# Down projections of two groups per feed-forward block: two of four pairs by seven products, added from PSUM to the residual; constants loaded per mixer

## The chip, the cores and the metric

The kernel runs on one core of one Trainium2 chip. The metric is device time in microseconds (us). Before the change it is 2205.03 us, the median of three runs between 2204.33 and 2206.0 us.

## The reference

Input is x, 512 tokens of 1024 channels, before which 16 learned meta tokens stand (528 tokens in all). Two layers (DEPTH = 2) each apply a feed-forward block, a mixer and a second feed-forward block:

```python
for l in range(DEPTH):
    h = h + 0.5 * swiglu(rmsnorm(h, norm_gains[l, 0]), ffn_w_gate[l, 0], ffn_w_up[l, 0], ffn_w_down[l, 0])
    h = h + mixer(rmsnorm(h, norm_gains[l, 1]), w_in[l], ...)
    h = h + 0.5 * swiglu(rmsnorm(h, norm_gains[l, 2]), ffn_w_gate[l, 1], ffn_w_up[l, 1], ffn_w_down[l, 1])
return rmsnorm(h, final_norm)[:, N_META:]

def swiglu(x, w_gate, w_up, w_down):
    return (jax.nn.silu(x @ w_gate) * (x @ w_up)) @ w_down
```

The inner width of a feed-forward block is 2816. The mixer joins a gated linear attention and a softmax attention. All of it is float32.

## The kernel before, in words

**Layout.** Channels lie on the 128 partitions, tokens on the free axis; the residual h stays on the chip as eight chunks of 128 channels by 528 tokens (`hall`). After the mixer of the last layer only the 512 real tokens are kept, so in the last feed-forward block a half of the tokens has 256 columns instead of 264. A float32 matmul is made of three: every operand is split into a high part (`hi`, rounded to the format `fp32r`) and a low part (`lo`, the remainder), and high x high, high x low and low x high are added in PSUM.

**Weights.** They come from DRAM in slabs of 128 x 1024 floats (512 KB). `Weights.fetch` loads up to six slabs ahead on SP's queue into three `raw` buffers; `Weights.make` converts up to four ahead: ScalarE casts to `whi` (L283), VectorE forms the remainder `wlo` (L284); there are four buffers of each. `fetch` and `make` set the order of the program; a scheduler then orders each engine's queue by that order and by its estimate of when operands and buffers are ready.

**Gate and up.** The 22 hidden chunks of a block are worked on as 11 pairs, in groups of 4, 4 and 3 (`GROUPS`). For a pair, the gate and up projections are done by a seven-product scheme in place of eight block products: rows of the input (even and odd chunks) and halves of the tokens are the two-by-two blocks of the one operand, the pair's two hidden chunks and the rows those of the weights. The products are named "1", "2", "5", "6", "7", "4", "3"; each has its own slab and takes 24 matmuls (L671). "1", "2" and "4" use slabs as they are; the others use sums of slabs that `Weights.sums` makes: a negated copy on ScalarE (L231) and transfers on POOL's queue that add what they carry to their target (L236). Buffers for that are three long ones (`wsa`) and three short ones (`wsb`). The seven sums of the input (`Norm.pair`) lie in `xc`.

**PSUM.** All eight banks are two pools of two tiles of two banks, `ss` and `s2`; pairs take turns between them. A product's result that is both used and added to further is copied from PSUM by ScalarE (`snapshot`, L683, three buffers `snap`), and VectorE adds a second accumulator to it (L692, L697, L701) in a buffer `c` (two of them, one per pair, taken at product "2").

**Hidden rows.** `hidden` scales the gate half by the norm's factor rs (L712), applies SiLU (L438) and multiplies it with the up half (L721); the up half is scaled by rs in the last group only (L719). Then the row is split into high and low (L443, L444), in 16 buffers `g`. A row m = 1 follows product "4", a row m = 0 product "3".

**Down.** After a group, `down` computes for each of the 8 output chunks the sum over the group's hidden chunks (L455 by `product`): 384 matmuls of half of the tokens for a group of four pairs, or 192 of all 512 tokens in the last block. In the first two groups `add_to_h` scales the result by rs into a buffer (L591) and adds that to h (L600); in the last group it adds from PSUM (L596). The first chunks begin before the last pair's hidden rows are ready, and take these last.

**The first block** differs at its start: pairs 0 and 1 use plain block products (`first_pair`, L625), while the sums of the input are still being made, and their four hidden rows follow together once rs is known.

**Constants.** Rotary tables, an identity and small matrices (721 KB, `ct`) and a mask are loaded once, on ScalarE's queue, during pair 5 of the first block (L388). The mixer begins with `decay_weights` (L1147 to L1151), which loads a 256 KB weight and splits it by a column of the constants; four gate rows with SiLU, the low-rank product (L1163) and two pairs of heads follow. Its first reader of the decay weights is the matmul in L813, which feeds the scan in L823.

Of the kernel before, what the change touches and what calls it, by code (L numbers as in the profile page):

```python
# [17 lines left out]
P = 128  # L18
# [24 lines left out]
GROUPS = (4, 4, 3)  # L43
HELD = 4
# [20 lines left out]
CONSTANTS_AT = 5  # L65
# [3 lines left out]
DIRECT = {"1": "11", "2": "12", "4": "22", **{b: b for b in BLOCKS}}  # L69


def ffn_steps(begin):
# [4 lines left out]
    for g, n in enumerate(GROUPS):  # L77
# [6 lines left out]
        for i in range(n):  # L84
            p, more = pair + i, i + 1 < n
            early = [[("P", p + 1, "1")], [("P", p + 1, "2")]] if more else \
                [[("D", g, 0, 0, 2 * n - 2)], [("D", g, 1, 0, 2 * n - 2)]]
            if begin and p < 2:
                continue
            if g == 0 and i == 0:  # L90
                early = [[], []]
            steps += early[0] + [("P", p, "7")] + early[1] + [("P", p, "4"), ("P", p, "3")]
            if more:
                steps += [("P", p + 1, "6"), ("P", p + 1, "5")]
# [7 lines left out]
def weight_plan():  # L102
# [8 lines left out]
    def ffn(l, f):  # L111
        for step in ffn_steps((l, f) == (0, 0)):
# [4 lines left out]
            elif step[0] == "F":  # L117
                plan.extend(("op", (l, f), step[1], step[2] + c) for c in "12")
            else:
# [41 lines left out]
NPAIR = FF // P // 2  # L161
# [39 lines left out]
class Weights:  # L201
# [3 lines left out]
    def __init__(self, nc, after, raw, hi, lo, wts, win):  # L205
        self.nc, self.raw, self.hi_pool, self.lo_pool, self.wts, self.win = nc, raw, hi, lo, wts, win
# [8 lines left out]
        self.made, self.fetched, self.got, self.summed, self.raws = 0, 0, {}, {}, {}  # L215
        self.pos, self.behind, self.after = 0, None, after

    def dram(self, f, i, name):
        return self.win[((f[0] * 2 + f[1]) * NPAIR + i) * 4 + BLOCKS.index(name)]

# [17 lines left out]
    def sums(self, f, i, product, w):  # L238
# [3 lines left out]
        if product == "1":  # L242
# [4 lines left out]
            got[f, i, "7"], got[f, i, "6"] = s3, s2  # L247
        else:
            s1 = self.block(f, i, "21", self.short, "wsb")
            self.add(s1, self.dram(f, i, "22"))  # L250
            s4 = self.negative(f, i, "s4", w)
            self.add(s4, got[f, i, "6"])
            got[f, i, "5"], got[f, i, "3"] = s1, s4
# [37 lines left out]
    def use(self, j):  # L291
# [3 lines left out]
        self.make(upto)  # L295
# [18 lines left out]
    def op(self, *load):  # L314

        assert PLAN[self.pos][1:] == load, (PLAN[self.pos], load)
        self.pos += 1
        return [t.rearrange("p (w k m) -> p w k m", w=2, k=KC // 2) for t in self.use(self.at[load])]


def build(tc, ctx, xt, wts, win, par, w2, const, umask, out):
# [16 lines left out]
    W = Weights(nc, after, pool("wraw", 3), pool("whi", 4), pool("wlo", 4), wts, win)  # L338
# [45 lines left out]
    ct = one.tile([P, NCONST], F32, name="const")  # L384
    mask = one.tile([P, P], U32, name="mask")
    nc.sync.dma_start(front[:, : KC + T], xt[:, : KC + T])
    def load_constants():
        S.dma_start(ct, const)  # L388
        S.dma_start(mask, umask)

# [3 lines left out]
    cos, sin = ct[:, C_COS : C_COS + T], ct[:, C_SIN : C_SIN + T]  # L394
    ident = ct[:, C_ID : C_ID + P]
# [6 lines left out]
    b64, diag2 = ct[:, C_B64 : C_B64 + P], ct[:, C_DIAG : C_DIAG + P]  # L402
# [190 lines left out]
    def add_to_h(m, acc, rs, f):  # L593
        if rs is None:
            for pv, cut in acc.parts:
                V.tensor_tensor(cut(h(m)), cut(h(m)), pv, ALU.add)  # L596
        else:
            t = slot("t")
            scaled(t, acc, rs, f)
            V.tensor_tensor(h(m), h(m), t, ALU.add)  # L600

    pending, kept = [load_constants], []

    def ffn(l, f, norm, done, following):
# [3 lines left out]
        pools = kept.pop() if kept else open_pools("left", psum=("s2",), c=2, snap=3, s2=2)  # L608
        made, hid, sums = {}, {}, {}

        def second(p):
            return (p + f) % 2 == 0

        factor = []

        def first_pair(p, m):
# [14 lines left out]
            if "c" not in st:  # L631
                st["c"] = slots["c"].tile([P, 4 * T], F32, tag="c", name=nm("c"))[:, : 4 * n] \
# [760 lines left out]
```

## Time and profile before

| | |
|---|---|
| runs | 2204.33, 2205.03, 2206.0 us |
| profiled execution, first to last instruction | 2203.2 us |
| matmuls | 16572 |
| slab casts by ScalarE (`whi`) | 219 + 190 + 84, about 1.05 us each |
| slab remainders by VectorE (`wlo`) | 219 + 190 + 84, about 1.22 us each |
| additive transfers on POOL's queue | 4 x 42, 512 KB each |

PE is TensorE's matmuls, PEld its weight loads, DVE VectorE, ACT ScalarE, POOL GpSimd, SP SyncE. A row of the chain in order of time gives start, duration and a run of like instructions. A row of the timeline gives start, duration, engine, line and operation, tiles written and read, sizes, count, and in brackets the idle time before it with what ended it. A row of groups gives the count, the busy time and mean ns of one, then the idle time just before. Feed-forward blocks lie at 0 to 372, 768 to 1122, 1122 to 1484 and 1849 to 2203 us; the mixers between.

### The profile page before, as it was taken

To read this page: it belongs to the slowest core of one execution; us is meant where nothing else is said; L and a number is where in the kernel's file an instruction comes from. 1 tells how busy PE (TensorE), PEld (TensorE's weight loads), DVE (VectorE), ACT (ScalarE), POOL (GpSimd) and SP (SyncE) were. 2 spreads that over 40 slices of the span, in tenths; PEclk is the share of its full clock that TensorE was granted. 3 is DMA by queue.
4 is the path that set the end of the run, shared out by engine and by line. 5 is a ranking of instruction groups with operands and counts; after the bars stand their busy time and mean duration, and the time that the engine had idled before them with its cause. 6 is when DMAs were issued, how large, how long until landed. Compare 5 with 4: busy or idle time off the path is not lost.

```text
span 2203.2 us, 39894 instructions
## 1 busy us (share of the span) xinstructions
PE 2184.4 (99%) x16572; PEld 2091.6 (95%) x16572; DVE 1510.3 (69%) x2401; ACT 1214.3 (55%) x1820; POOL 147.3 (7%) x172
## 2 busy tenths in 40 slices
PE   9999999999999999999999999999999999999998
PEld 9999999999999999999999999999888888989897
DVE  7656567577876686565786575675879867656565
ACT  8535355355784574453585363554557847536354
POOL 0011000000000010101010110000000001101010
PEclk9999999999999999999999999999999999999999
DMA  8578553211113585866677685632211146868562
GB/s 251 156 177 228 145 143 111 80 60 65 39 39 125 133 224 151 197 168 174 174 186 194 172 211 147 160 110 78 68 66 60 40 134 165 237 158 225 148 168 67
DMA packets 87286, 310.22 MB, mean 141 GB/s; under 512 B 9665, under 2 KB 11841, under 8 KB 87105
## 3 DMA queue, kind: packets, MB, share of 16 engines
q1 hardware_dynamic: 61120, 217.15, 28.8%
q0 software_dynamic: 24192, 88.09, 23.0%
q8 instruction: 130, 2.13, 0.4%
q10 hardware_dynamic: 1792, 2.43, 0.4%
q14 instruction: 52, 0.42, 0.1%
HBM read 261.50 MB, written 2.10 MB: 120 GB/s over the span
## 4 chain that ended last, share of the span: by engine, by line
PE 91%; DVE 6%; ACT 2%; issue 1%; DMA 0%; DVEq 0%; SPq 0%; ACTq 0%
PE ss L671 38%; PE ss L455 28%; PE mm L455 13%; PE sm L455 3%; PE ss L625 2%; PE sm L1083 1%; PE ss L653 1%; PE ss L1057 1%; DVE wlo L284 1%; ACT t L438 1%; PE sm L1101 1%; PE sm L1102 1%; PE ss L1058 1%; DVE t L823 1%; PE sm L899 0%
## 5 line engine op out<-in xcount | busy, mean ns | idle before, releaser
L671 PE MATMUL ss<-xc,whi 128*128 128x264 f32 (+1 forms) x4608 | 837.3, 284 | 0.0
L671 PEld LDWEIGHTS ss<-xc,whi 128*128 128x128 f32 x4608 | 711.9, 188 | 1.3 <-ACT snap L683 0.5
L671 PE MATMUL ss<-xc,wlo 128*128 128x264 f32 (+1 forms) x2304 | 651.8, 283 | 0.0
L455 PE MATMUL ss<-g,whi 128*128 128x264 f32 (+1 forms) x2620 | 482.5, 300 | 0.0
L671 PEld LDWEIGHTS ss<-xc,wlo 128*128 128x128 f32 x2304 | 433.7, 188 | 0.0
L455 PEld LDWEIGHTS ss<-g,whi 128*128 128x128 f32 x2620 | 380.7, 188 | 15.6
L455 PE MATMUL mm<-x,whi 128*128 128x264 f32 (+1 forms) x1712 | 384.1, 314 | 0.0
L283 ACT CAST whi<-w 128x1024 fp32r<-128x1024 f32 (+1 forms) x219 | 228.8, 1046 | 240.6 <-PE ss L455 116.3
L283 ACT CAST whi<-raw 128x1024 fp32r<-128x1024 f32 x190 | 199.1, 1048 | 263.1 <-PE ss L671 89.7
L284 DVE TENSOR_TENSOR wlo<-w,whi 128x1024 fp32r<-128x1024 f32 (+1 forms) x219 | 265.6, 1217 | 105.0 <-ACT whi L283 102.0
L455 PE MATMUL ss<-g,wlo 128*128 128x264 f32 (+1 forms) x1310 | 301.9, 300 | 0.0
L284 DVE TENSOR_TENSOR wlo<-raw,whi 128x1024 fp32r<-128x1024 f32 x190 | 232.0, 1221 | 90.8 <-ACT whi L283 89.0
L455 PEld LDWEIGHTS mm<-x,whi 128*128 128x128 f32 x1712 | 279.0, 189 | 15.5 <-DVE x L444 0.2
L455 PE MATMUL mm<-x,wlo 128*128 128x264 f32 (+1 forms) x856 | 264.4, 313 | 0.0
L455 PEld LDWEIGHTS ss<-g,wlo 128*128 128x128 f32 x1310 | 209.1, 188 | 8.3
L283 ACT CAST whi<-s 128x1024 fp32r<-128x1024 f32 x84 | 88.2, 1050 | 145.1 <-PE ss L671 126.7
L455 PEld LDWEIGHTS mm<-x,wlo 128*128 128x128 f32 x856 | 160.1, 189 | 7.1
L284 DVE TENSOR_TENSOR wlo<-s,whi 128x1024 fp32r<-128x1024 f32 x84 | 102.7, 1223 | 91.7 <-ACT whi L283 91.7
L231 ACT ACTIVATE s<-w 128x1024 f32<-128x1024 f32 x84 | 89.1, 1061 | 78.8 <-DMA w<-win 49.0
L591 DVE SCALAR_TENSOR_TENSOR t<-ss,rs 128x528 f32<-128x528 f32 (+1 forms) x64 | 44.3, 700 | 126.9 <-PE ss L455 126.8
L236 POOL DMA_DIRECT2D w<-win x42 | 37.0, 882 | 963.4 <-DVE g L1214 739.8
L683 ACT COPY snap<-ss 128x528 f32<-128x528 f32 (+1 forms) x126 | 73.8, 586 | 1.6 <-PE ss L671 1.6
(287 smaller groups left out, 2883.3 us busy)
## 6 DMA issues: line engine op xcount, KB each, us to landing
w<-win SPq DMA_DIRECT2D x217, 512.0 KB, 4.9
raw<-wts SPq DMA_DIRECT2D x190, 512.0 KB, 3.4
w<-win POOLq DMA_DIRECT2D x42, 512.0 KB, 7.6
s<-win POOLq DMA_DIRECT2D x42, 512.0 KB, 6.8
w<-s POOLq DMA_DIRECT2D x42, 512.0 KB, 5.5
s<-w POOLq DMA_DIRECT2D x42, 512.0 KB, 6.6
h<-xt SPq DMA_DIRECT2D x7, 264.0 KB, 5.7
const<-const ACTq DMA_DIRECT2D x1, 721.0 KB, 9.3
```

Of the source, the lines that this page charges most:

```text
L231: self.nc.scalar.activation(t, w, AF.Copy, scale=-1.0)
L236: self.nc.gpsimd.dma_start(t, src, accum_op=ALU.add)
L283: nc.scalar.copy(hi[:, cs], w[:, cs])
L284: nc.vector.tensor_tensor(lo[:, cs], w[:, cs], hi[:, cs].bitcast(F32), ALU.subtract)
L438: prev_act[0] = S.activation(*args, **kw).ins
L455: TE.matmul(acc.half[i][:width], lhs, rhs[:, acc.spans[i]], start=first, stop=last)
L591: V.scalar_tensor_tensor(cut(dst[rows]), pv[rows], -0.5 * f, cut(rs[rows]), ALU.mult, ALU.mult)
L625: last = TE.matmul(acc[:, t, :w], a[:, j, k], v[b][:, r], start=k == 0 and r == 0 and i == 0, stop=k == len(x) - 1 and r == 1 and i == 2)
L653: TE.matmul(acc[:, j], a[:, j, k], b[:, at], start=k == 0 and i == 0, stop=k == last and i == 2)
L671: TE.matmul(acc[:, j], a[:, j, k], b[:, at], start=bool(begin and k == 0 and i == 0), stop=k == len(x) - 1 and i == 2, skip_group_check=no ...
L683: snap = S.copy(st[name], acc).ins
L823: V.tensor_tensor_scan(c[:, bs], ones.broadcast_to([P, n]), g[:, bs], 0.0, ALU.mult, ALU.add)
```

## The change

In the first two groups of every feed-forward block, the first two pairs' share of the down projection is done by seven products too, with the same forms: output rows (even and odd chunks) and halves of the tokens are the blocks. Their hidden rows are not split as they are, but as the seven forms (`forms`), in `g` and a new pool `gx` of six buffers in place of the three `snap`. The other two pairs' share is done by plain products over four slabs per group (`oa`, `ob`, `ea`, `eb`). One group's down stage has eleven steps in the order `SEVEN`, from eleven slabs instead of eight, of which four are sums made as for the gate and up products, with four more additive transfers. Step "1" stands before the last pair's products "4" and "3". Every accumulator is added from PSUM to two chunks of h at a time (`add`, 16 per group), so the hidden rows of all pairs are now scaled by rs in the up half. Copies from PSUM go straight into `c`, which is taken at product "1". The order of the third pair's product "3" and the fourth's "6" is exchanged. The third group and the closing part stay, but for the buffers of the squares. Constants and mask are loaded at the start of each mixer into its own pools, and `decay_weights` moves behind the gate rows and the table load.

```diff
 GROUPS = (4, 4, 3)
+SEVENS = 2
+SEVEN = ("1", "6", "5", "7", "o22", "4", "o21", "ea", "2", "eb", "3")
-CONSTANTS_AT = 5
+SUMMED = [sum(GROUPS[:g]) + i for g in range(SEVENS) for i in range(2)]
...
+            if g < SEVENS and not more:
+                steps += [("P", p, "7"), ("S", g, "1"), ("P", p, "4"), ("P", p, "3")]
+                steps += [("S", g, what) for what in SEVEN[1:]]
+                continue
...
+            if g < SEVENS and i == n - 2:
+                steps += [("P", p, "4"), ("P", p + 1, "6"), ("P", p, "3"), ("P", p + 1, "5")]
...
-        self.make(upto)
+        self.last = j
+        self.make(upto - self.hold)
...
-        pools = kept.pop() if kept else open_pools("left", psum=("s2",), c=2, snap=3, s2=2)
+        pools = kept.pop() if kept else open_pools("left", psum=("s2",), c=2, gx=6, s2=2)
...
-            def snapshot(name):
-                t = slots["snap"].tile([P, T], F32, tag="snap", name=nm("snap"))[:, :n]
-                st[name] = v2(t)
+            def snapshot(q):
                 with tc.high_priority():
-                    snap = S.copy(st[name], acc).ins
+                    snap = S.copy(st["c"][:, :, q], acc).ins
...
             if product == "1":
-                snapshot("p1")
+                st["c"] = quarters()
+                snapshot(0)
...
             for _, ud, _, us, cs in cuts:
-                if p >= NPAIR - GROUPS[-1]:
-                    V.scalar_tensor_tensor(ud, us, -0.25, rs[:, cs], ALU.mult, ALU.mult)
-                    us = ud
-                V.tensor_tensor(ud, t[:, cs], us, ALU.mult)
-            hid[2 * p + m] = split(u, "g", "g")
+                V.scalar_tensor_tensor(ud, us, -0.25, rs[:, cs], ALU.mult, ALU.mult)
+                V.tensor_tensor(ud, t[:, cs], ud, ALU.mult)
+            if p in SUMMED:
+                st["rows"] = st.get("rows", 0) + 1
+                if st["rows"] == 2:
+                    formed[p] = forms(c)
+            else:
+                hid[2 * p + m] = split(u, "g", "g")
+
+        def forms(c):
+            t, u = c[:, 0], c[:, 1]
+            two = [[v2(slot(tag, F32R)) for _ in range(2)] for tag in ("g", "g", "gx")]
+            last = v2(slot("gx", F32R))
+            def parts(to, src):
+                S.copy(to[0], src)
+                V.tensor_tensor(to[1], src, to[0].bitcast(F32), ALU.subtract)
+            parts(two[0], u[:, 0:4:2])
+            V.tensor_tensor(t[:, 0:4:2], u[:, 1:2].broadcast_to([P, 2, w]), u[:, 0:4:3], ALU.subtract)
+            V.tensor_tensor(t[:, 1], u[:, 3], t[:, 0], ALU.subtract)
+            parts(two[1], t[:, 0:2])
+            V.tensor_tensor(t[:, 3], u[:, 2], t[:, 1], ALU.subtract)
+            parts(two[2], t[:, 2:4])
+            S.activation(last[:, 0], u[:, 3], AF.Copy, scale=-1.0)
+            V.scalar_tensor_tensor(last[:, 1], u[:, 3], -1.0, last[:, 0].bitcast(F32), ALU.mult, ALU.subtract)
+            return [(hi[:, i], lo[:, i]) for hi, lo in two for i in range(2)] + [(last[:, 0], last[:, 1])]
+
+        def seven(g, what):
+            base, (left, right) = sum(GROUPS[:g]), (slice(0, w), slice(w, n))
...
+            def times(to, half, name, wt, begin=False):
+                hi, lo = wt
+                for k in range(2):
+                    xh, xl = formed[base + k][PLACE[name]]
+                    for j in range(2):
+                        for i, (a, b) in enumerate(((hi, xh), (hi, xl), (lo, xh))):
+                            TE.matmul(to[:, j], a[:, 2 * half + j, k], b, start=begin and k == 0 and i == 0,
+                                      stop=k == 1 and i == 2, skip_group_check=not begin)
+
+            def plain(to, hs, wt, begin=False):
+                hi, lo = wt
+                for k in range(4):
+                    xh, xl = hid[2 * base + 4 + k]
+                    for j in range(2):
...
+            def add(src, half, row, hs):
+                to = hall[:, 4 * half + row : 4 * half + 4 : 2, hs]
+                with tc.high_priority():
+                    V.tensor_tensor(to, to, src, ALU.add)
+
+            if what in ("1", "6", "7", "4"):
+                W.hold = 2 * (what == "4")
+                wt = weights(what)
+                for half in range(2):
+                    x = acc("x", half, (not alone) if what == "1" else None)
+                    times(x, half, what, wt, what == "1")
+                    if what != "4":
+                        add(x, half, *{"1": (0, left), "6": (0, right), "7": (1, right)}[what])
+            elif what == "5":
...
+            elif what == "o22":
+                st["odd"] = []
+                for half in range(2):
+                    W.hold = half
+                    st["odd"].append(weights(PLAINS[half]))
+                    plain(acc("z", half), right, st["odd"][half])
+                    add(acc("z", half), half, 1, right)
...
-        pools = open_pools("left", e=8, i=5, p=7, q=6, k=5, lr=1, w2=1)
+        pools = open_pools("left", e=8, i=5, p=7, q=6, k=5, lr=1, w2=1, ct=1, mk=1)
+        load_constants()
         banks = open_pools("left", psum=("mm", "sm"), mm=2, sm=2)
-        w2t = decay_weights(l)
...
         table("natural_log_exp_and_others")
+        w2t = decay_weights(l)
```

More of the change, by code (lines that the diff above doesn't have):

```diff
@@ L201, with __init__ @@
 class Weights:
[L205 to L206 removed]
+    def __init__(self, nc, after, raw, hi, lo, wts, win, wdn):
+        self.nc, self.raw, self.hi_pool, self.lo_pool, self.wts, self.win, self.wdn = nc, raw, hi, lo, wts, win, wdn
+        self.hold, self.last = 0, 0
         self.long = self.short = None
@@ L317, in op, with build @@
         self.pos += 1
-        return [t.rearrange("p (w k m) -> p w k m", w=2, k=KC // 2) for t in self.use(self.at[load])]
-def build(tc, ctx, xt, wts, win, par, w2, const, umask, out):
+        w = 2 if load[1] < NPAIR or load[2] in PLAINS else 4
+        return [t.rearrange("p (w k m) -> p w k m", w=w, m=P) for t in self.use(self.at[load])]
+def build(tc, ctx, xt, wts, win, wdn, par, w2, const, umask, out):
     nc = tc.nc
@@ L336, in after @@
         return tc.issue_after(ins) if ins is not None else nullcontext()
-    W = Weights(nc, after, pool("wraw", 3), pool("whi", 4), pool("wlo", 4), wts, win)
+    W = Weights(nc, after, pool("wraw", 3), pool("whi", 4), pool("wlo", 4), wts, win, wdn)
     pss = pool("pss", 2, bass.MemoryType.PSUM)
@@ L591, in scaled, with add_to_h @@
             V.scalar_tensor_tensor(cut(dst[rows]), pv[rows], -0.5 * f, cut(rs[rows]), ALU.mult, ALU.mult)
[L593 to L602, printed above, removed]
+    def add_to_h(m, acc):
+        for pv, cut in acc.parts:
+            V.tensor_tensor(cut(h(m)), cut(h(m)), pv, ALU.add)
+    kept = []
     def ffn(l, f, norm, done, following):
@@ L738, in down @@
                 return
-            with tc.high_priority() if g == len(GROUPS) - 1 and m >= KC - 2 else nullcontext():
-                add_to_h(m, sums[m], rs if g < len(GROUPS) - 1 else None, 0.5)
-            if g == len(GROUPS) - 1:
-                (done or finish_chunk)(m)
+            with tc.high_priority() if m >= KC - 2 else nullcontext():
+                add_to_h(m, sums[m])
+            (done or finish_chunk)(m)
         steps = ffn_steps((l, f) == (0, 0))
@@ L766, in ffn @@
                 two_products(*step[1:])
+            elif step[0] == "S":
+                seven(*step[1:])
             else:
@@ L1240, in closing @@
         last = {}
-        squares = [slots["snap"].tile([P, T], F32, tag="snap", name=nm("square")) for _ in late]
+        squares = [slots["gx"].tile([P, T], F32, tag="gx", name=nm("square")) for _ in late]
         table("natural_log_exp_and_others")
@@ L1364 @@
     win = np.ascontiguousarray(gu.transpose(0, 1, 6, 7, 4, 5, 2, 3, 8)).reshape(-1, P, SLAB)
+    dn = a["ffn_w_down"].reshape(DEPTH, 2, NPAIR, 2, P, KC // 2, 2, P)
+    parts = []
+    for l in range(DEPTH):
+        for f in range(2):
+            for g in range(SEVENS):
+                p = sum(GROUPS[:g])
+                for row in range(2):
+                    for c in range(2):
+                        parts.append(dn[l, f, p : p + 2, c, :, :, row].transpose(1, 2, 0, 3).reshape(P, SLAB))
+                for row in (1, 0):
+                    for half in range(2):
+                        js = slice(2 * half, 2 * half + 2)
+                        parts.append(dn[l, f, p + 2 : p + 4, :, :, js, row].transpose(2, 3, 0, 1, 4).reshape(P, SLAB))
+    wdn = np.ascontiguousarray(np.stack(parts))
     par = np.zeros((P, NPAR), np.float32)
```

123 lines of the change are left out of this document (89 added, 34 removed).

## The prediction

> **What bounds the kernel now.** I read the busy shares first, then the chain of waits, then who waits for whom on TensorE's weight loads, then stretches.
>
> ```profile
> span 2203.2 us, 39894 instructions
> PE 2184.4 (99%) x16572; PEld 2091.6 (95%) x16572; DVE 1510.3 (69%) x2401; ACT 1214.3 (55%) x1820; POOL 147.3 (7%) x172
> PEclk9999999999999999999999999999999999999999
> PE 91%; DVE 6%; ACT 2%; issue 1%; DMA 0%; DVEq 0%; SPq 0%; ACTq 0%
> PEld ss L671 <- ACT snap L683: 0.3, 2, 0.2
> ```
>
> TensorE is busy for 99% of the span at full clock, and the chain that ends last runs over it for 91%. The last row is the whole list of waits of its weight loads from 768 to 1484 us, two complete feed-forward blocks: 0.3 us. Feed-forward blocks are one unbroken stream of matmuls, so here a matmul less is its whole time less, as long as nobody else comes late. The pace comes from the chain in order of time (start, duration, piece):
>
> ```profile
> 141.38 73.10 PE ss L671 x600
> 103.38 38.00 PE ss L455 x312
> 1973.43 70.75 PE ss L671 x600
> 1937.32 36.12 PE ss L455 x156
> ```
>
> In the first three blocks a 264-column matmul takes 73.10/600 = 0.1218 us in the gate/up products and 38.00/312 = 0.1218 us in the down projections. In the last block 512 tokens are live: a gate/up matmul has 256 columns and takes 70.75/600 = 0.1179 us, and a down matmul has all 512 and takes 36.12/156 = 0.2315 us.
>
> **Matmuls removed.** A group of four pairs has 8 hidden chunks by 8 output chunks by 3 (high/low) by 2 halves = 384 down matmuls of 264 columns. After: seven products of 24 (2 pairs x 2 halves x 2 columns x 3) = 168 for the two summed pairs, and 4 steps of 48 = 192 for the two plain ones; 360 in all. That saves 24 x 0.1218 = 2.92 us per group, in six groups 17.5 us. In the last block the new code halves the columns everywhere: before 192 x 0.2315 = 44.45 us, after 360 x 0.1179 = 42.44 us, so only 2.0 us per group, 4.0 us in two. Sum: **-21.5 us** if nothing is exposed.
>
> [...]
>
> **VectorE (DVE) work added.** Prices of back-to-back instructions, from 52.91 us, 58.80 us and the 264-wide ones at 28 us, and by form:
>
> ```profile
> 52.91 2.56 DVE L712 SCALAR_TENSOR_TENSOR c<-c,rs 128x528 f32<-128x528 f32 x4
> 58.80 1.32 DVE L721 TENSOR_TENSOR c<-c 128x528 f32<-128x528 f32 x2
> 28.23 0.42 DVE L544 TENSOR_TENSOR t<-t 128x264 f32<-128x264 f32 x1
> 28.58 0.42 DVE L547 TENSOR_TENSOR t<-t,t 128x264 f32<-128x264 f32 x1
> L284 DVE TENSOR_TENSOR wlo<-w,whi 128x1024 fp32r<-128x1024 f32 x17 | 20.7, 1224 | 9.8 <-ACT whi L283 9.2 <-PE ss L671 0.2
> L591 DVE SCALAR_TENSOR_TENSOR t<-ss,rs 128x528 f32<-128x528 f32 (+1 forms) x64 | 44.3, 700 | 126.9 <-PE ss L455 126.8
> L600 DVE TENSOR_TENSOR h<-h,t 128x528 f32<-128x528 f32 (+1 forms) x64 | 44.1, 700 | 1.2
> ```
>
> A 528-wide one takes 0.64 us, a 264-wide one 0.35 us, a weight remainder (`wlo`) 1.22 us. Per block:
> - the up half of the first eight pairs is now scaled by rs: 0.64 + 2 x 0.35 = 1.33 us per pair, 10.6 us;
> - `forms` of a summed pair: three 528 remainders, one 528 and two 264 differences, one 264 negation, 4 x 0.64 + 3 x 0.35 = 3.6 us, against two remainders (1.3 us) before: +2.3 us, four pairs, 9.2 us;
> - six more slabs (11 for 8 in two groups), 7.3 us;
> - 32 additions from PSUM to the residual, 0.70 us each, in place of 16 scalings (L591) and 16 additions (L600) at 0.70 us: nothing.
>
> That is 27 us per block, 108 us in all, DVE from 69% to some 74%. ScalarE (ACT) has 55% and gets per block ten casts and negations of slabs at 1.05 us and four pairs' copies, about 1.1 us each: 15 us, 60 in all, to 58%; it is the lighter of the two. Whether DVE's additions reach TensorE depends on the stretch (stretch, length, then busy of PE, PEld, DVE, ACT, POOL, clock, DMA share, GB/s):
>
> ```profile
> 141.40:214.48 73.08, 73.08 (x602) 73.08 (x602) 50.72 (x61) 43.43 (x57) 9.61 (x11) 1.00 0.85 216
> 232.00:270.00 38.00, 38.00 (x316) 38.00 (x315) 20.69 (x27) 12.57 (x14) 4.36 (x5) 1.00 0.71 167
> 768.00:842.00 74.00, 74.00 (x607) 73.82 (x607) 59.99 (x80) 53.58 (x72) 9.82 (x12) 1.00 0.84 214
> 768.40:788.00 19.60, 19.60 (x163) 19.60 (x162) 18.72 (x28) 17.51 (x26) 1.74 (x2) 1.00 0.68 172
> 54.00:85.00 31.00, 31.00 (x257) 31.00 (x256) 25.56 (x33) 22.59 (x31) 3.49 (x4) 1.00 0.76 190
> ```
>
> In a later group's gate/up products DVE goes from 50.72 by 4 x 1.33 + 2 x 2.3 = 9.9 us to 60.6 of 73.1 us, 83%: covered, since a slab is cast three products (8.8 us) ahead. In the down stage (20.69 of 38.00 us, 54%) there is room for the casts. At the start of blocks two to four it goes from 59.99 by 3 x 1.33 + 2 x 2.3 = 8.6 us to 68.6 of 74.0 us, 93%. DVE has stood 18.72 of 19.60 us, 95%, there without TensorE waiting, so I take 0.5 us per block, 1.5 us (bounds 0 and 3.6 us each, the first pair's own additions).
>
> **Where it is exposed: the first block after its first two pairs.** There all four hidden rows come at once, 25.56 of 31.00 us are taken, and 2 x 1.33 + 2 x 2.3 = 7.3 us are added: 32.9 in 31.0 us. And the new code copies the first product of pair 2 into a `c` buffer, where a `snap` buffer stood; there are two `c`, so the copy waits until `forms` of pair 0 has read its own.
>
> ```profile
> 53.69 32.18 PE ss L671 x264
> 58.18 0.71 DVE L444 TENSOR_TENSOR g<-c,g 128x528 fp32r<-128x528 f32 x1 [0.23 <-ACT g L443]
> 57.02 0.60 ACT L683 COPY snap<-ss 128x528 f32<-128x528 f32 x1
> ```
>
> Pair 0's `c` was done with at 58.18 + 0.71 = 58.9 us; after, 1.3 + 2.3 = 3.6 us later, 62.5, and the copy (0.60) ends at 63.1 us. Product 6 of pair 2 adds onto the PSUM that is being copied, and is due two products after 53.69: 59.5 us. TensorE would wait 3.6 us, unless pair 3's first product, which goes to the other PSUM pool, is ordered ahead of it (one product is 2.9 us). I take **+3 us**; bounds 0 and 7.3 us (all that is added there).
>
> **The joint inside a group.** The last pair's product 3 is followed by its hidden row, whose reader stands three products (6, 5, 7: 3 x 2.92 us) and 12 matmuls (1.5 us) later: 10.2 us. Before, product 3 ended at 987.83 and the row was ready at 992.76 + 0.70:
>
> ```profile
> 987.83 37.91 PE ss L455 x312
> 992.76 0.70 DVE L444 TENSOR_TENSOR g<-c,g 128x528 fp32r<-128x528 f32 x1
> ```
>
> That is 5.6 us, in which two slabs were converted too; the new scaling (0.64) and three additions with priority (3 x 0.70) make 8.4 us. 1.8 us are left, so I take 0.5 us for the eight groups together; bounds 0 and 1 us each, were one more slab remainder (1.22 us) and one more addition queued ahead. The residual additions wait for TensorE in DVE's queue; the slab remainders stand behind them, with the 8.8 us of lead.
>
> **Weights.** Each group now has its own chain of sums on POOL's queue (four accumulating transfers) and one more load on SP's. The chain, and how long it takes (a product 1 of a pair in the steady state):
>
> ```profile
> 914.09 1.06 ACT L231 ACTIVATE s<-w 128x1024 f32<-128x1024 f32 x1 [0.79 <-DVE wlo L284]
> 915.56 0.89 POOL L236 DMA_DIRECT2D s<-win  x1 [7.91 <-ACT s L231]
> 921.37 0.87 POOL L236 DMA_DIRECT2D w<-s  x1 [4.92 <-DMA s<-win]
> 920.54 1.05 ACT L283 CAST whi<-w 128x1024 fp32r<-128x1024 f32 x1 [1.88 <-PE ss L671]
> w<-s POOLq DMA_DIRECT2D x42, 512.0 KB, 5.5
> ```
>
> From the negation to the sum: 921.37 - 914.09 + 5.5 = 12.8 us. It starts 6.5 us before product 1 is cast, which is 8.8 us before product 1 runs; the new step 6 comes three products, 8.8 us, after step 1. Lead 24 us less 12.8 less a conversion of 2.3 leaves 9 us: nothing. For transfers as a whole:
>
> ```profile
> q1 hardware_dynamic: 61120, 217.15, 28.8%
> q0 software_dynamic: 24192, 88.09, 23.0%
> ```
>
> One of 414 slab loads takes 0.288 x 2203/414 = 1.5 us of all engines, one of 168 accumulating ones 0.230 x 2203/168 = 3.0 us. A group gets 1.5 + 4 x 3.0 = 13.5 us more; the stretches 141-214 (0.85) and 232-270 (0.71) show room in 126 us for it.
>
> **Constants.** The 721 KB now go to each mixer's start on ACT's queue, with the two decay-weight transfers behind the gates' table load:
>
> ```profile
> const<-const ACTq DMA_DIRECT2D x1, 721.0 KB, 9.3
> 372.94 5.35 PE sm L455 x44
> 390.02 3.86 PE sm L1163 x32
> 422.32 1.36 DVE t L823 x5
> ```
>
> Their first reader is the decay weights near 391 us, whose own first reader feeds the scan at 422 us; the mixer starts at 372. 9.3 us fit into 19, and two issues of 0.35 us are all that ACT pays. If the buffer came free late, the casts behind the issue have 3 slabs of lead. I take 0, bounds -2 and +4 us for both mixers, as their order around the scans shifts.
>
> **Sum.** -21.5 + 1.5 (starts) + 3 (first block) + 0.5 (joints) + 0 (weights, constants) = -16.5 us. The profiled span is 2203.2 us, the median of the runs 1.8 us more, 2205.03: 2186.7 for the span, **2188.5 us** for the median.
>
> **Rivals.**
> - Nothing is exposed (the waiting product is overtaken, DVE keeps up): -21.5, **2183.5 us**. For it: 95% DVE without a wait. Against it: 32.9 us of work in 31.0.
> - DVE becomes the bound in summed pairs, the case on the other side. `forms` hands over to ACT three times, and the slab remainders behind it stand in the same queue. Such a pair has 50.72/73.08 x 20.45 + 1.33 + 2.3 = 17.8 us of DVE in 20.45. The 18.5 us left of the gain are eaten at 1.16 us for each of 16 pairs, that is when DVE can't hold more than 17.8/21.6 = 82%. At 78% a pair takes 22.8 us: 16 x 2.4 = +38 us, **2224 us**. For it: the present share there is 69%; against it the 95% over 19.6 us.
> - Weight sums late. Were landings at the longest of those transfers, 11.6 us, the chain would take 1.06 + 0.4 + 23.2 + 2.3 = 27 us against 24: 3 us in half of eight groups, +12, **2200 us**. For it: a DMA share of 0.85; against it the median.
>
> ```profile
> DMA to landing us min/median/max: 4.5/6.0/11.6
> ```
>
> - The mixers lose by the moved constants: +4 and the joints +4, **2196 us**.
> - The narrow matmuls of the last block are paced by their weight loads. A whole load each would be 360 x 0.188 = 67.7 us a group for 44.45 before: +47 us in two, **2235 us**; the 0.1179 us row all but excludes it. [...]
>
> ```profile
> L671 PEld LDWEIGHTS ss<-xc,whi 128*128 128x128 f32 x4608 | 711.9, 188 | 1.3 <-ACT snap L683 0.5
> ```
>
> **How the numbers follow.** Forecast 60% (own range 2184 to 2196), nothing exposed 17%, DVE bound 10%, sums late 7%, mixers 5%, narrow matmuls 1%. No change within what can be told apart is 0.2%, 4.4 us: 2200.6 to 2209.4. Faster: 60 + 17 + 5 + a bit of the sums, 83%; same 7%; slower 10%. The range runs from the full gain with the mixers' -2 (2182) to the late sums (2202); the DVE bound is left out.
>
> **What would show it.** Right: down steps at 0.12 us a matmul without gaps; one wait of about 3 us near 60 us for a copy by ACT, weight loads waiting for nothing else in later blocks. Wrong: waits of weight loads for `wlo` in summed pairs (DVE bound), ACT casts waiting for DMA in the down stages (sums), idle TensorE near 372 us or 420 us (constants).

## The result, and the profile after

| | before | after |
|---|---|---|
| median of the runs (us) | 2204.68 (2204.15 to 2206.0) | 2243.45 (2241.11 to 2247.82) |
| ratio, with its 95% interval | | 1.0178 [1.0165, 1.019] |
| profiled execution, span (us) | 2203.2 | 2239.3 |
| granted clock over the span | 0.998 | 0.989 |

Medians and ranges here and below leave out two executions in a slower state: one of the version with both orders (2993 us) and one of the kernel before beside a later experiment (5991 us).

The kernel became 1.8% slower: 2243.45 us against a forecast of 2188.5 with a range of 2182 to 2202. The profiled execution is 36.1 us longer, where 16.5 us less were forecast. Its page begins so (busy time and share of each engine):

```profile
span 2239.3 us, 40811 instructions
PE 2183.8 (98%) x16764; PEld 2104.0 (94%) x16764; DVE 1611.1 (72%) x2599; ACT 1267.9 (57%) x1892; POOL 175.6 (8%) x204
```

TensorE is busy as long as before (2183.8 against 2184.4 us), though by the forecast's count it has 21.5 us less to do at full clock. Two things have taken the place of that gain: TensorE stands, and it runs slower. Who waits for whom (total us, times, longest):

```profile
PE ss L695 <- ACT c L705: 37.1, 9, 6.0
ACT whi L305 <- DMA w<-s: 54.2, 8, 8.5
```

Line 695 is a gate/up product, line 705 the copy from PSUM to `c`, line 305 a slab's cast. The first of the nine waits is that of the first block which the forecast named: 3.86 us, up to 64.58 us. The other eight, 33.3 us together, come once in each group of seven products: 3.08 us up to 101.35, 3.24 up to 230.50, 4.98 up to 862.11, 3.44 up to 993.96, 5.41 up to 1224.03, 3.87 up to 1356.23, 5.98 up to 1957.82 and 3.26 up to 2085.99. The second row, also eight times, is ACT's own wait for a weight sum. In order of time, in the second block (start, duration, engine, line, and in brackets the idle time before and what ended it):

```profile
840.49 1.05 ACT L251 ACTIVATE s<-w 128x1024 f32<-128x1024 f32 x1
845.28 0.89 POOL L256 DMA_DIRECT2D w<-wdn  x1 [11.19 <-DVE wlo L306]
845.84 1.24 POOL L256 DMA_DIRECT2D s<-wdn  x1
855.93 0.87 POOL L256 DMA_DIRECT2D w<-s  x1 [8.85 <-DMA s<-wdn]
860.52 1.04 ACT L305 CAST whi<-w 128x1024 fp32r<-128x1024 f32 x1 [7.61 <-DMA w<-s]
861.47 0.59 ACT L705 COPY c<-ss 128x528 f32<-128x528 f32 x1
862.11 0.81 PE L695 MATMUL ss<-xc,whi 128*128 128x264 f32 x2 [4.98 <-ACT c L705]
```

Read from below: product 4 of the last pair (862.11) adds onto the PSUM that the copy of product 7 (861.47) has to read first. The copy's data had been there for seven microseconds (product 7's last matmul ends at 854.24), but it stands in ACT's queue behind the cast of step 6's sum, and that cast waited 7.61 us for a transfer. The transfer (`w<-s`, s2 += s3) was issued at 855.93, when s3's had landed; and s3's was issued at 845.84, though its negation was done at 841.54, because s1's (`w<-wdn`) stood ahead of it on POOL's queue and waited for a buffer that the remainder of an earlier slab (L306) still read.

Then the clock. Stretches of the same kernel: length, then busy time and instructions of PE, PEld, DVE, ACT and POOL, granted clock, DMA share and GB/s. The seven rows in the middle are all that run at half clock between the first block's wait and the end; the first and the last stand for comparison:

```profile
101.35:106.00 4.65, 4.65 (x38) 4.65 (x39) 4.65 (x9) 1.97 (x2) 0.00 (x0) 1.00 0.02 4
229.38:236.21 6.83, 5.71 (x26) 5.71 (x27) 4.91 (x8) 2.21 (x4) 0.00 (x0) 0.50 0.14 40
860.85:867.68 6.83, 5.57 (x25) 5.57 (x26) 4.89 (x7) 2.22 (x4) 0.00 (x0) 0.50 0.10 31
993.97:997.38 3.41, 3.41 (x15) 3.41 (x16) 3.41 (x5) 0.89 (x1) 0.00 (x0) 0.50 0.00 0
1222.66:1229.49 6.83, 5.46 (x25) 5.46 (x26) 4.89 (x7) 2.27 (x3) 0.00 (x0) 0.50 0.10 22
1355.78:1359.19 3.41, 2.96 (x13) 2.97 (x14) 3.41 (x5) 1.34 (x2) 0.00 (x0) 0.50 0.00 0
1956.53:1963.36 6.83, 5.54 (x26) 5.54 (x27) 4.83 (x8) 2.36 (x4) 0.00 (x0) 0.50 0.10 32
2086.23:2089.64 3.41, 3.41 (x18) 3.41 (x18) 3.41 (x6) 0.65 (x1) 0.00 (x0) 0.50 0.00 0
867.68:871.00 3.32, 3.32 (x29) 3.32 (x28) 2.96 (x6) 1.89 (x3) 0.86 (x1) 1.00 0.26 99
```

After seven of the eight waits the granted clock is 0.50 for 3.41 or 6.83 us. What that costs a matmul shows in the timeline, ahead of the wait and behind it; from one of these rows to the next three matmuls start:

```profile
853.22 0.29 PE L695 MATMUL ss<-xc,wlo 128*128 128x264 f32 x1
853.59 0.29 PE L695 MATMUL ss<-xc,wlo 128*128 128x264 f32 x1
862.72 0.42 PE L695 MATMUL ss<-xc,wlo 128*128 128x264 f32 x1
863.38 0.42 PE L695 MATMUL ss<-xc,wlo 128*128 128x264 f32 x1
```

A matmul of 264 columns takes 0.66/3 = 0.220 us there, where it takes 0.37/3 = 0.123 at full clock (0.1218 over long stretches), so 45% of the time at half clock is lost. TensorE is busy in these seven stretches for 5.71 + 5.57 + 3.41 + 5.46 + 2.96 + 5.54 + 3.41 = 32.1 us, of which 14.3 us are lost. Only after the wait of 3.08 us (first row of the stretches) the clock stays full. Waits and clock together, 33.3 + 14.3 = 47.6 us, are what the eight late sums cost by this count; what the change would be without them, the experiments show.

### The profile page after: what moved, and what is told of

The parts are those of the page before. It is cut to its first block, busy times and chain, and to the rows that moved or that the text cites. A ratio compares the mean times of both kernels' runs of the same rounds, so it can differ in the third digit from the quotient of the medians.

```text
span 2239.3 us, 40811 instructions
## 1 busy us (share of the span) xinstructions
PE 2183.8 (98%) x16764; PEld 2104.0 (94%) x16764; DVE 1611.1 (72%) x2599; ACT 1267.9 (57%) x1892; POOL 175.6 (8%) x204
## 5 line engine op out<-in xcount | busy, mean ns | idle before, releaser
L695 PE MATMUL ss<-xc,whi 128*128 128x264 f32 (+1 forms) x4608 | 853.1, 287 | 37.2 <-ACT c L705 37.1
L306 DVE TENSOR_TENSOR wlo<-w,whi 128x1024 fp32r<-128x1024 f32 (+1 forms) x259 | 315.2, 1217 | 207.8 <-ACT whi L305 207.3
L305 ACT CAST whi<-w 128x1024 fp32r<-128x1024 f32 (+1 forms) x259 | 269.9, 1045 | 229.5 <-PE ss L695 114.4
L305 ACT CAST whi<-raw 128x1024 fp32r<-128x1024 f32 x126 | 132.0, 1048 | 152.6 <-PE mm L482 69.5
L306 DVE TENSOR_TENSOR wlo<-raw,whi 128x1024 fp32r<-128x1024 f32 x126 | 153.9, 1222 | 80.1 <-ACT whi L305 79.0
L797 PE MATMUL ss<-g,whi 128*128 128x264 f32 (+1 forms) x1024 | 186.6, 283 | 0.0
L251 ACT ACTIVATE s<-w 128x1024 f32<-128x1024 f32 x100 | 106.0, 1060 | 132.0 <-DMA w<-win 83.0
L306 DVE TENSOR_TENSOR wlo<-s,whi 128x1024 fp32r<-128x1024 f32 x100 | 122.2, 1222 | 71.9 <-ACT whi L305 70.7
L797 PEld LDWEIGHTS ss<-g,whi 128*128 128x128 f32 x1024 | 158.2, 188 | 0.0
L482 PE MATMUL ss<-g,whi 128*128 128x264 f32 (+1 forms) x828 | 153.1, 301 | 0.0
L797 PE MATMUL ss<-g,wlo 128*128 128x264 f32 (+1 forms) x512 | 145.0, 283 | 0.0
L482 PEld LDWEIGHTS ss<-g,whi 128*128 128x128 f32 x828 | 120.5, 188 | 5.2
L710 DVE TENSOR_TENSOR c<-c,ss 128x528 f32<-128x528 f32 (+1 forms) x126 | 87.8, 697 | 41.5 <-ACT c L705 33.2
```

The lines of the kernel that those rows point to most:

```text
L251: self.nc.scalar.activation(t, w, AF.Copy, scale=-1.0)
L305: nc.scalar.copy(hi[:, cs], w[:, cs])
L306: nc.vector.tensor_tensor(lo[:, cs], w[:, cs], hi[:, cs].bitcast(F32), ALU.subtract)
L482: TE.matmul(acc.half[i][:width], lhs, rhs[:, acc.spans[i]], start=first, stop=last)
L695: TE.matmul(acc[:, j], a[:, j, k], b[:, at], start=bool(begin and k == 0 and i == 0), stop=k == len(x) - 1 and i == 2, skip_group_check=no ...
L710: V.tensor_tensor(st["c"][:, :, q], st["c"][:, :, q], acc, ALU.add)
```

## The experiments

Theory 1 is the reading above: a late sum blocks ACT's queue, the copy behind it stops TensorE, and each pause costs part of a slow stretch as well. Theory 2 is the forecast's rival on the other side: VectorE with its added work, or its two `c` buffers, is the bound in summed pairs, and the copies would come late in any case. The kernel before, run beside them, had medians of 2204.3 to 2204.6 us.

**POOL's order.** s1's transfer is issued behind the two that step 6 needs.

```diff
-            self.add(s2, s3)
+            second = self.add(s2, s3)
...
-            self.add(s1, self.dram(f, i, "22"))
+            with self.after(second if product == "1" else None):
+                self.add(s1, self.dram(f, i, "22"))
...
```

> Edit: in the weight sums of each group's seven products, the accumulating transfer of s1 (needed by step 5) is issued on POOL's queue behind that of s2 (needed by step 6), where it stood ahead of s3's, on which s2 waits. Nothing else. Theory 1 (the late sum): the cast of step 6's sum waits 5.7 to 8.5 us for its transfer at the head of ACT's queue, the copy of product 7 behind it is late and TensorE stands 3.1 to 6.0 us in each of eight groups (33.3 us), and each time some 2.3 us more go at a lower granted clock. Before s3's transfer stood 5.4 us of POOL's queue (845.84 for a negation done at 841.5), and s3 then landed in 10 us beside s1's, where such a transfer takes 5.5 us alone: step 6's sum comes 8 to 10 us earlier, the eight waits go (at most 0 to 8 us of them stay), TensorE's copy waits fall from 37.1 us to about 4 (the one at 64 us), span about 2239.3 - 33.3 - 18 = 2188 us (2185 to 2197). Theory 2 (VectorE's new work is the bound in summed pairs, or its two `c` buffers are): the copies still come late, the waits stay at 25 us or more, span 2230 to 2243.

Measured: 2201.63 us (2197.21 to 2203.95), ratio 0.9986 [0.9977, 0.9995]; span 2195.4 us in the profiled execution, which is its fastest run. Its waits:

```profile
PE ss L696 <- ACT c L706: 7.0, 4, 3.9
```

And the same place in time:

```profile
832.45 0.89 POOL L256 DMA_DIRECT2D s<-wdn  x1 [7.48 <-ACT s L251]
840.81 0.87 POOL L256 DMA_DIRECT2D w<-s  x1 [7.48 <-DMA s<-wdn]
846.56 1.05 ACT L306 CAST whi<-w 128x1024 fp32r<-128x1024 f32 x1 [3.14 <-DMA w<-s]
847.51 0.59 ACT L706 COPY c<-ss 128x528 f32<-128x528 f32 x1
1919.64 0.51 PE L696 MATMUL ss<-xc,whi 128*128 128x256 f32 x2 [2.41 <-ACT c L706]
```

The waits fall from 37.1 to 7.0 us, 3.87 of them in the first block, and the span by 43.9 us: theory 2 is out as the cause of the loss. But the sum came only 4.5 us earlier, not 8 to 10: the negation was at 830.99, so from there to the cast it is 15.6 us, where it was 20.0. s3's transfer, alone on POOL, still took 7.48 us (7.28 in the last block's first group). The cast waits 3.14 us even here, and 0.51 us of that reach TensorE; in the last block it is 2.41 us, and 3.41 us at half clock from 1920.83. No margin is left, so it depends on each transfer: the runs spread over 6.7 us.

**ACT's order.** The sums stay late; the cast of step 6 goes behind the copy.

```diff
+                if q == 3 and p + 1 in (GROUPS[0], sum(GROUPS[:2])):
+                    W.joint = snap
...
+                if not isinstance(load, int) and load[1] >= NPAIR and load[2] == "6":
+                    held = self.joint
...
```

> Edit: ACT's cast of step 6's sum is ordered behind the copy of the last pair's product 7, which it preceded. The sums stay as late as they are. Theory 1: the copy comes at once, product 4 runs through, and TensorE meets the late sum only at step 6, two products later: in the second block the sum is cast at 860.52 + 1.04 and the remainder follows by 862.9, while step 6 would be due at 862.11 - 4.98 + 2 x 2.92 = 863.0: no wait there; in the last block 1958.6 against 1957.5, a wait of up to 1 us. So the eight waits of 33.3 us become 0 to 6 us in all, on weight loads and no more on the copy, and the clock keeps full: 2188 to 2195 us. If the queue of ACT had nothing to do with it and the sum itself were what TensorE lacks, the waits would only move to step 6 and stay at 25 us or more: 2230 to 2243. Theory 2 (VectorE): no change, 2235 to 2243.

Measured: 2206.59 us (2203.12 to 2210.13), ratio 1.001 [1.0, 1.002]; span 2207.9. From the waits of its profile:

```profile
PE ss L698 <- ACT c L708: 3.9, 1, 3.9
PE ss L802 <- DVE h L808: 3.0, 5, 1.5
PE ss L793 <- DVE wlo L309: 1.5, 2, 0.8
ACT whi L308 <- DMA w<-s: 42.9, 9, 8.0
```

ACT waits for the sums nearly as long as before (42.9 us), but the eight waits for the copy are gone, and 31.4 us of the span with them. So the queue of ACT is where the late sum turned into the large loss. The expectation missed the time by 13 us: the late slab is now met in small pieces at step 6 and behind it (casts and remainders, and additions from PSUM that VectorE does late; the granted clock over the span is 0.997). The waits of TensorE in this profile sum to some 9 us beyond the first block and beyond those of the kernel before; the rest of the 18.3 us by which it lies above the run without sums (below) isn't attributed wait by wait.

**Both orders.** The two edits above in one kernel.

> Edit: both orders, that of POOL's transfers and that of ACT's cast behind the copy. Theory 1: one wait is left, near 64 us (3.9 us, for the copy into `c` in the first block, with its slower clock behind it), span 2185 to 2190; if the order on POOL alone removes all waits, the same as that run within 2 us. Theory 2: 2230 or more.

Measured: 2197.58 us (2194.85 to 2198.33), ratio 0.9967 [0.9954, 0.9979]; span 2196.5, above the 2185 to 2190 expected; one large wait, 3.87 us up to 64.04. The two orders together are better than POOL's alone by 4 us in the median, so the second isn't superfluous.

**Both orders, and pair 3's first product early.**

```diff
-            steps += [("F", p, m) for p in (0, 1) for m in "12"] + [("P", 2, c) for c in "1265"]
+            steps += [("F", p, m) for p in (0, 1) for m in "12"] + [("P", 2, c) for c in "12"]
+            steps += [("P", 3, "1")] + [("P", 2, c) for c in "65"]
...
```

> Edit: both orders, and in the first block pair 3's first product runs ahead of product 6 of pair 2, one product (2.9 us) to stand in the wait of 3.9 us near 64 us. If that wait is a copy that comes late because `c` is still read, it falls to about 1 us and with it most of the slower clock behind it: 4 to 6 us less than with both orders alone, 2180 to 2185, about the full gain of 21.5 us with what the block starts cost. If VectorE is simply behind there, the wait comes again one product later and nothing is gained: 2185 to 2190.

Measured: 2192.80 us (2190.26 to 2195.59), ratio 0.9948 [0.9933, 0.9962]; span 2188.1, 8.4 us less than with both orders in the profiled executions, 4.8 in the medians, but above the 2180 to 2185 expected. The wait for the copy is gone from the list; in its place stands a shorter one, for a slab's cast, and 3.41 us at half clock behind it (from 64.92):

```profile
PE ss L702 <- ACT whi L312: 1.2, 1, 1.2
```

**No sums at all.** The changed kernel with its own orders, each group's accumulating transfers left out (`add` returns at once where its new argument is true). The expectation speaks of three; the edit leaves out all four, those of s3, s2, s1 and s4, and POOL's additive transfers fall back to 4 x 42:

```diff
-            self.add(s3, self.dram(f, i, "21"))
+            self.add(s3, self.dram(f, i, "21"), i >= NPAIR)
...
```

> Edit, in the changed kernel with its own orders: the three accumulating transfers by which each group's seven products get summed weights are left out (s3 without B21, s2 without s3, s1 without B22; all loads, negations, conversions and products stay), so the down projections of the summed pairs are computed with other weights. Theory 1: nothing of ACT waits at the head of its queue for a sum, the eight waits are gone, the first block's one stays: 2239.3 - 33.3 - 19 (seven and more stretches at half clock) = 2187 us, 2184 to 2191, and as no transfer runs late, the runs lie close together (within 2 us). Against it a rival on what is left behind the order of POOL's queue: if the remaining 7 us of that version (2195.4) and its scatter of 7 us come from VectorE or the mixers and not from transfers, this run stays at 2193 to 2200 with the same scatter. Theory 2 (VectorE is the bound in summed pairs): 2230 or more, since all its work is kept.

Measured: 2191.97 us (2191.82 to 2192.32), ratio 0.9944 [0.993, 0.9959]; span 2189.6, within the 2184 to 2191 of theory 1. VectorE has all its work (1612.6 us busy), and there is one wait for a copy, 3.9 us. So these transfers, late as they are, cost 2239.3 - 2189.6 = 49.7 us, 2 us more than the 47.6 counted above; most of the 2 us lie at the edges of the pauses (a pause is counted from the end of the matmul ahead of it, some 0.16 us after the next would have started). The runs lie within 0.5 us, so the spread of the others comes with these transfers. This run also prices the rest of the change. From the chains of the kernel before and of this one (start, duration, piece):

```profile
767.86 5.85 PE ss L653 x48
1483.86 4.66 PE sm L455 x20
1849.12 5.66 PE ss L653 x48
```

```profile
373.53 5.88 PE sm L483 x48
768.09 5.86 PE ss L678 x48
1471.46 5.59 PE sm L483 x24
1838.55 5.69 PE ss L678 x48
```

Mixers begin with such an `sm` piece (the row of before for the first, 372.94 + 5.35, stands in the prediction; the ends are compared, since some of its matmuls are missing), blocks two and four with an `ss` piece of 48:

| stretch | before | no sums | difference | forecast |
|---|---|---|---|---|
| first block, to 378.29 / 379.41 | 378.29 | 379.41 | +1.1 | -5.84 + 3 + 0.1 = -2.7 |
| first mixer, to 767.86 / 768.09 | 389.57 | 388.68 | -0.9 | 0 |
| blocks two and three, to 1488.52 / 1477.05 | 720.66 | 708.96 | -11.7 | -11.7 + 1.0 + 0.25 = -10.4 |
| second mixer, to 1849.12 / 1838.55 | 360.60 | 361.50 | +0.9 | 0 |
| last block, to the end | 354.08 | 351.05 | -3.0 | -4.0 + 0.5 + 0.1 = -3.4 |

**A plain first group in the first block.** As the version with both orders and the early product, with seven products in seven groups.

```diff
+def sevens_in(block):
+    return (1,) if block == (0, 0) else (0, 1)
...
-            if p in SUMMED:
+            if p in SUMMED and p >= sum(GROUPS[: sevens_in((l, f))[0]]):
...
```

> Edit: as the version with both orders and pair 3's first product early, and the first group of the first block gets the four plain pairs of before (16 more slabs of plain weights are read there, seven products in seven groups only). Theory 1: that group's gain of 2.9 us is given up, and with it goes what its forms cost between 60 and 70 us, where the version with seven products in all eight groups still waits 1.2 us and then runs 3.4 us at half clock (some 4.4 us of the first block's 5.8 are lost there). Span 2185 to 2188, no waits at 60 to 70 us, and less scatter of the runs if the first block causes it. Rival: the loss near 65 us is of another cause (VectorE's slab conversions): then it stays, and the span is about 2191.

Measured: 2193.07 us (2191.71 to 2193.61), ratio 0.9948 [0.9931, 0.9964]; span 2191.4. TensorE waits 0.2 us in all from 50 to 380 us, and the granted clock over the span is 0.999 (0.998 in the version with the early product), as theory 1 had it, but the time is no better, and its later groups have small waits for VectorE's additions. A stretch around step 6 in the second block, in this version and in the one without sums (columns as above):

```profile
849.50:866.00 16.50, 16.37 (x132) 15.97 (x131) 16.46 (x24) 7.38 (x9) 0.87 (x1) 1.00 0.49 131
```

```profile
851.00:867.50 16.50, 16.50 (x137) 16.50 (x136) 15.04 (x22) 8.18 (x10) 0.89 (x1) 1.00 0.58 154
```

With sums VectorE is busy for 16.46 of 16.50 us and TensorE lacks five matmuls; without them VectorE has 1.5 us to spare. The two stretches don't begin at the same matmul, so they are close, not equal, in what they hold. That a late cast bunches VectorE's work there fits the two rows; it wasn't tried by itself.

**An earlier start of the chain.** The negation of step 1's slab ordered one conversion earlier, in three versions: both orders with the early product; the same without ACT's order; and with a plain first group.

```diff
...
+            ahead = self.loads[s + 1] if s + 1 < len(self.loads) else 0
+            if not isinstance(ahead, int) and ahead[1] >= NPAIR and ahead[2] == "1":
+                self.fetch(s + 2)
+                self.sums(*ahead, self.raws[s + 1])
```

> Edit: as the version with both orders and pair 3's first product early; besides, the negation of step 1's slab and with it each group's chain of sums starts one slab conversion (one product, 2.9 us) earlier. Theory 1: the late sums are what is left between that version (2188.1 us in its profiled execution, 2190.3 to 2195.6 in its runs) and the one without accumulating transfers, so the cast of step 6's sum stops waiting (it waited 3 to 5 us in the version with POOL's order alone), and the runs come down to 2185 to 2190 us and lie closer together. The rival: the buffers of the sums (three of each kind) are still held by the sums before, so the chain can't start earlier, and nothing changes: 2190 to 2196.

> Edit: the same without the order on ACT's queue (the cast of step 6's sum stands ahead of the copy of product 7 again). Theory 1: if the sum is there in time, its place in ACT's queue costs nothing: the same time as with that order within 2 us. If the sums still come late in some groups, copies wait again, 1 to 3 us each with a stretch at half clock: 2193 to 2202.

> Edit: as the first of these three, with four plain pairs in the first block's first group. If the late sums were the cause of the 5 us by which the profiled execution of the version with a plain first group (2191.4 us) lay above its sum of terms (-21.5 + 2.9 + 1.5 + 0.5 = -16.6 us from 2203.2: 2186.6), this one comes to 2185 to 2189; if VectorE's dense stretches behind step 6 are it, it stays at 2190 to 2193.

Measured: 2193.31 (2191.97 to 2195.54), ratio 0.995 [0.9933, 0.9966]; 2198.04 (2194.71 to 2203.87), ratio 0.9971 [0.9961, 0.998]; 2194.11 (2192.71 to 2194.88), ratio 0.9953 [0.9938, 0.9968]. Nothing gained, but the edit didn't do what it was for: in the first of them the negation stands at 828.67, at 828.36 in the version without the edit, both right behind the cast of the same slab. So whether an earlier chain would bring more is open. The second shows that the order on ACT's queue is still worth 4.7 us in the median: without it five copies wait again, 3.4 us.

**How long a pause has to be.** In the kernel before, the copy of product 7 in each group's last pair is repeated.

```diff
...
+                    for _ in range(STALL[2 * l + f][groups_up_to(p) - 1] if name == "r" and last else 0):
+                        S.copy(st[name], acc)
                     snap = S.copy(st[name], acc).ins
```

> Edit, in the kernel before: in the last pair of each of the twelve groups the copy of product 7 from PSUM, onto which product 4 adds, is repeated 7 to 15 times more at 0.6 us each; a down step of 4.4 us lies between, so that TensorE should stand from about 0.7 us (7 times) to 5.5 us (15 times). The output stays the same. Theory 1, on the price of a wait: after waits of about 3.2 us and more the granted clock is a half for a stretch of 3.4 or 6.8 us, as eight of nine waits of the changed kernel show (3.08 us: none; 3.24 to 5.98 us: 3.41 or 6.83 us), shorter waits are followed by full speed and cost only themselves; so 3 to 6 of the twelve are followed by half clock and the span grows by the sum of the waits and about 1.7 to 3.4 us for each of these. The rival: the clock falls after any pause, also one of 1 to 2 us, so that all twelve are followed by a slow stretch; or it never does, and the slower matmuls of the changed kernel have another cause: the span then grows by the waits alone.

Measured: span 2286.8 us (2288.61 for the execution), 83.6 more than before. Its waits:

```profile
PE ss L678 <- ACT snap L693: 59.1, 13, 8.9
```

The twelve are longer than planned, 2.43 to 8.89 us, 58.8 in all. Each of them is followed by half clock, for 3.41 (from 101.79) to 10.24 us (from 1122.38), 68.3 in all, 19.1 of which lie within the waits themselves; the granted clock over the span is 0.983. With 45% of the rest of the slow time lost it is 58.8 + 0.45 x (68.3 - 19.1) = 80.9: waits and clock are nearly the whole growth in this one execution. The pauses that separate the two are in other runs: after 2.41 us (above) there was a slow stretch, after 3.08 us in the changed kernel there was none. So neither form of the expectation holds; the last section sets pauses and slow stretches side by side.

## Why the prediction was wrong

**The step that failed** is the paragraph on weights: "Lead 24 us less 12.8 less a conversion of 2.3 leaves 9 us: nothing." Three things in it were off.

- *The deadline.* The lead was counted to the matmuls of step 6. But the cast is issued three products ahead, and behind it in ACT's queue stands the copy of product 7, which ran right behind it, at 861.47, though its data had been there since 854.24. ACT reached the cast at 860.52 - 7.61 = 852.9 us, 12.4 us after the negation, and TensorE needed the copy at 862.11 - 4.98 = 857.1. From the start of the cast to TensorE, cast and copy take 862.11 - 860.52 = 1.6 us, which leaves 857.1 - 840.5 - 1.6 = 15.0 us for a chain of 12.8: 2.2 us to spare by the forecast's own numbers, not 9. The forecast said itself that "a slab is cast three products (8.8 us) ahead", and it asked what stands behind DVE's waiting additions, but not what stands behind a waiting cast in ACT's queue. The run with ACT's order shows this step alone.
- *The chain.* It took 20.0 us, not 12.8: 3.9 us more before s3's transfer is issued (behind s1's on POOL's queue), 4.3 more until it lands beside s1's, 0.9 less for the second. The change moved s1's transfer from product 2 to step 1, where the program has it behind the other two and the scheduler put it ahead of them on POOL's queue; the forecast took the chain of a pair, where it isn't. The row it took was also a quick one: before the change POOL waited for s3's transfer for 4.92 us there, but for 269.4/42 = 6.4 us on average (row below). With POOL's order mended the chain is 15.6 us, half a microsecond over the 15.0, and the copy comes 0.51 us late.
- *The price.* The rival "weight sums late" (7%, 2200 us) was the right mechanism, and the forecast named its sign, ACT casts waiting for DMA in the down stages. It was priced at 3 us in half of eight groups. It came in all eight, with 3.1 to 6.0 us, and each but one drew half clock behind it: 49.7 us for the forecast's 12. That a wait costs more than its length was in no term of the sum.

The row of the kernel before for the chain, POOL's wait for the transfer into s3 (total us, times):

```profile
DMA s<-win: 269.4, 42
```

**What held.** The matmuls removed: blocks two and three gain 11.7 us without sums, exactly 4 x 2.92, and the last block 3.0 of 4.0 (where the missing 1.0 went isn't known; it has no new wait). Narrow matmuls lose nothing: they start 0.118 us apart there (8.51 us for 72 down matmuls in the run without sums), as forecast. VectorE isn't the bound: with 1612.6 us of work in all it adds no wait to blocks two to four, so the 1.5 us for the block starts and the 0.5 for the joints weren't needed either. The constants: -0.9 and +0.9 us in the two mixers, together the 0 forecast, but partly by luck. The first mixer of the kernel before has 3.41 us at half clock (from 558.01) that the run without sums doesn't have (granted clock over the span 0.998 in both, though this one has a slow stretch near 65 us), some 1.5 us; without it the mixers lose about 1.5 us (an estimate). The wait at `c` in the first block came where it was placed and for 3.87 us, where 3.6 was worked out and 3 taken; there too the clock was missing, 3.41 us at half, 1.5 us, and 1.6 us more went in small pieces: with the wait 7.0 instead of 3 us. The forecast's total, in which late sums cost nothing, is -16.5; the run without sums is at -13.6; the first block lost 3.9 us against its forecast, and the rest gained 1.0.

The fastest version that computes the reference, both orders with the early product, takes 0.9948 [0.9933, 0.9962] of the time before: the change is worth 0.5%, once three places in the order of issue are right. The run without sums stands at 0.9944, 0.8 us lower, with 3.9 + 1.5 us of the first block's wait still in it, of which this version has 1.2 + 1.5 left; like with like, the late sums still cost this version some 3.5 us (an estimate).

## What to carry to other kernels

A transfer's lead ends where the first instruction that waits for it stands in its engine's queue, not where its data is used; look up what else stands behind that instruction, and who waits for that (here the place of one cast in ACT's queue was worth 31.4 us of the span). When a change moves a transfer onto a queue, time the chain with what is then ahead of it, and not from the rows in which nothing was. And price a pause of TensorE with the slow stretch that may follow it: here seven of eight waits of 3.08 to 5.98 us had one, which cost 1.3 to 2.6 us more (45% of the 2.96 to 5.71 us that TensorE was busy in it).

## What the runs showed of the hardware

**Pauses and half clock.** In each of three profiles the slow stretches begin whole steps of 3.413 us apart: in the changed kernel at 65.54, at 229.38 (48 steps later), at 860.85 (185 more); in the kernel before at 558.01 and at 2196.41, its last (480 steps); in the run with longer pauses at 101.79 and 1122.38 (299). So each profile is cut here into windows of one such step, and TensorE's pauses are summed by window.

| profile | at full clock, from 10 us on: pauses in a window (us) | the next window |
|---|---|---|
| changed kernel | 2.12 (from 225.97), 2.45 (from 62.13), 2.70 (from 2229.60), 3.17 (from 2082.82), 3.40 and more (five windows) | half clock |
| changed kernel | 1.28, 1.40, 1.52 and 1.67 (from 1949.70, 96.27, 58.72 and 99.68); 1.02 at most in the others | full clock |
| kernel before | 2.59 (from 2193.00) | half clock |
| kernel before | none (from 554.60) | half clock |
| kernel before | 1.03 at most in all others | full clock |
| pair 3's first product early | 1.38 (from 61.51: the wait of 1.24 us and 0.14 of the next) | half clock |

The window from 554.60 is in a mixer, and two rows of eight matmuls of 2 columns stand in it. The wait of 3.08 us lies in the windows from 96.27 and 99.68, 1.40 us in the one and 1.67 in the other. As 1.38 us was followed by half clock and 1.40 to 1.67 us were not, no single sum divides the windows. Where a window was itself at half clock, 1.11 to 1.37 us of pauses were followed by another at half (from 229.38, 860.85, 1222.66 and 1956.53), 0.45 us by full clock (from 1355.78). So the wait that ends at 862.11, of which 1.26 us lie in the slow window, had 6.83 us at half, and the one that ends at 1356.23 had 3.41.

**An accumulating transfer beside others.** From the end of its issue to POOL's next one, s3's took 7.48 and 7.28 us in two groups of the run with POOL's order, where s1's was issued behind it, and 6.89 to 9.74 us in the eight groups of the changed kernel, beside s1's. From issue to landing, the medians of the changed kernel's accumulating transfers are 6.1 to 9.2 us (six rows of 8 to 50); those of its plain loads of the same 512 KB are 3.4 to 6.6 us.
